# Input projection by stripes of 512 weight columns in a ring of weight pairs, with two token slots instead of three

## The chip, the cores and the metric

One core of a Trainium2 chip runs the whole kernel in one launch. The metric is the time on the device in microseconds; smaller is better. TensorE is called PE, VectorE DVE, ScalarE ACT, GpSimd POOL, and SyncE, which issues most DMAs, SP.

## What is computed

One inference step of a hybrid trunk: a layer norm, one wide input projection of 2064 prompt rows (16 learned meta rows and 2048 tokens) and of 8 x 16 sample rows, two token mixers, gates and an output projection. Cut to what matters:

```python
(g_q, g_k, g_v, g_low, g_r, d_q, d_k, d_v, i_q, i_k, i_w, d_z, m_a, m_b) = jnp.split(
    h @ w_in, SPLIT_OFFSETS, axis=-1)             # h: rows x 1024, w_in: 1024 x 8280
...
log_f = jax.nn.log_sigmoid(g_low @ gla_w2 + gla_gate_b) / GLA_TAU
o_a, s_t = gla_recurrence(q, k, v, log_f, s0)     # linear attention, 4 heads
y_a = (rms_norm(o_a) * jax.nn.silu(g_r)) @ w_gla
...
k_i = layer_norm(i_k, idx_kn_g, idx_kn_b)
o_b = attend(q_d, q_i, w_i, k_d, v_d, k_i)        # index scores choose the 256 best keys, 16 heads
y_b = (o_b * jax.nn.silu(d_z)) @ w_dsa
merged = jax.nn.sigmoid(m_a + gate_b[0]) * y_a + jax.nn.sigmoid(m_b + gate_b[1]) * y_b
h_new = layer_norm(ALPHA * h + merged @ w_out, ln_g, ln_b)
```

Everything is fp32. The matmuls of the projections take each operand as a pair `hi`, `lo` of fp32r tiles (`hi` the rounded value, `lo` the rest), and make three products per contraction tile: hi·hi, hi·lo and lo·hi.

## The kernel before, in words

**Phase 1** (`phase1`, L549) holds the tokens as six pieces of three tiles of 128 (`PIECES`; the first has the 16 meta rows and two tiles, the last ends with the sample tile `s`). `phase_keys` (L356) normalises, transposes and splits each piece into `xh`, `xl` and computes the attention and index keys. Then `project` (L577) runs for three groups of two pieces, [4, 5], [2, 3] and [0, 1]. A group loads its pieces back from DRAM where they are not in a slot any more (L581 to L587: four raw loads of two contraction tiles each; a cast to `xh` on ACT and a subtraction to `xl` on POOL, in `split_sb`, L234). The slots are three pools `xp0` to `xp2`; the list `slots` (L568) says which piece takes which, and `xtiles` (L385) takes the next entry.

Within a group the 1024 x 256 **stripes** of `w_in` follow each other. `weights` (L239) loads a stripe in four raw loads, casts each to `whi` (ACT, L158) and subtracts to `wlo` (POOL, L143); `whi` and `wlo` hold all eight contraction tiles and have two buffers each, `raw` has three. Two kinds of product use them:

- weight-stationary, `stripe_t` (L389) with `tsp` (L304): 128 weight columns are stationary, a piece of 256, 272 or 384 tokens moves. For iq, gq, gk, q, ma and mb; written out by `evac` on ACT or DVE.
- token-stationary, `natural` (L591) with `nat` (L295): a token tile is stationary, the 256 weight columns move. For gv, gr and z.

A product has 24 matmuls (`mm3`, L260, lines 264 to 266). A group has two iq stripes, then 26 steps in the order of `order`; the tiles' index scores (`index_block`, L432, L444 and L445 on PE, reading `iq` from DRAM) come ahead of each set of steps, and the selections on DVE (`select`) at a later priority beside them. `flip` reverses the order of the pieces in the last stripe of the second group.

**Phase 2** (`phase2`, L1233) is attention, linear attention, the merge and the output. Linear attention's gates (`gla_gates`, L652) and the attention of the sample (`attend_sample`, L1122) are side work: its first `NEARLY` = 13 items are issued at a priority 1500 earlier, beside the end of phase 1, as far as their memory is free. The pools of phase 2 lie in SBUF over those that phase 1 leaves, the slots `xp` among them. A scheduler orders the instructions of each engine by these priorities and a model of the timeline, and so the final order isn't to be read off the source alone.

Of the kernel before, what the change touches and what calls it, by code (L numbers as in the profile page):

```python
# [21 lines left out]
P = 128  # L22
# [59 lines left out]
PMAX = 3 * P  # L82
SCW = KT * 300
# [35 lines left out]
class Trunk:  # L119
    def __init__(self, tc, i, o):  # L120
        self.tc, self.nc, self.i, self.o = tc, tc.nc, i, o
        self.turn = 0
        self.spare = self.flip = False
# [106 lines left out]
    def raw(self, n):  # L230
        t = self.ws.tile([P, 2 * PMAX], F32, name="raw", bufs=3)
        return t[:, : 2 * n].rearrange("p (k c) -> p k c", k=2)
# [6 lines left out]
    def weights(self, parts, pool=None, name="", eng=None):  # L239

        nc = self.nc
        width = sum(n for _, n in parts)
        w = self.i["w_in"][0].rearrange("(k p) c -> p k c", p=P)
        if pool is None:
            hi = self.ws.tile([P, KT, width], F32R, name="whi")
            lo = self.ws.tile([P, KT, width], F32R, name="wlo")
        else:
            hi = pool.tile([P, KT, width], F32R, name="whi" + name, tag="sc")
            lo = pool.tile([P, KT, width], F32R, name="wlo" + name, tag="sc")
        for q in range(4):  # L250
            s = slice(2 * q, 2 * q + 2)
            raw = self.raw(width)
            a = 0
            for c, n in parts:
                nc.sync.dma_start(raw[:, :, a : a + n], w[:, s, c : c + n])
                a += n
            self.split_sb(hi[:, s, :], lo[:, s, :], raw, eng)
        return hi, lo
# [36 lines left out]
    def nat(self, x, c, r, w):  # L295

        ps = self.pp.tile([P, 512], F32, name="pp")
        (hi, lo), (xh, xl) = w, x
        n = hi.shape[-1]
        self.mm3(ps[:r, :n], lambda k: xh[:, k, c : c + r], lambda k: xl[:, k, c : c + r],  # L300
                 lambda k: hi[:, k, :], lambda k: lo[:, k, :], KT)
        return ps[:r, :n]

    def tsp(self, x, c, n, w, a):  # L304

        ps = self.pp.tile([P, 512], F32, name="pp")
        (hi, lo), (xh, xl) = w, x
        self.mm3(ps[:, :n], lambda k: hi[:, k, a : a + P], lambda k: lo[:, k, a : a + P],
                 lambda k: xh[:, k, c : c + n], lambda k: xl[:, k, c : c + n], KT)
        return ps[:, :n]  # L310
# [78 lines left out]
    def stripe_t(self, g, c0, width, meta, evac):  # L389
        w = self.weights([(c0, width)])  # L390
        for q in GROUPS[g][:: -1 if self.flip else 1]:
            s = META if q == 0 and not meta else 0
            for a in range(0, width, P):
                evac(c0 + a, self.tsp(self.x[q], s, PCN[q] - s, w, a), PC0[q] + s, PCN[q] - s)
# [154 lines left out]
    def phase1(self):  # L549
        nc, tc, i = self.nc, self.tc, self.i  # L550
        with ExitStack() as c:
# [7 lines left out]
            self.xp = [c.enter_context(tc.tile_pool(name=f"xp{q}", bufs=1)) for q in range(3)]  # L559
# [9 lines left out]
            self.x, self.slots = {}, [0, 1, 2, 0, 1, 2, 0, 1, 2, 1]  # L569
# [7 lines left out]
    def project(self, g):  # L577
# [10 lines left out]
        for q in range(2):  # L588
            self.stripe_t(g, C_IQ + 256 * q, 256, False, self.ev_split("ih", "il", C_IQ))

        def natural(col, dst, base, meta, evac):  # L591
            w = self.weights([(col, 256)])
            for t, q in tiles:
# [5 lines left out]
                evac(e[:r, :256], ps)  # L599
                nc.sync.dma_start(self.d[dst][COL[t] : COL[t] + r, col - base : col - base + 256], e[:r, :256])  # L600
# [4 lines left out]
        def silu_norm(e, ps):  # L605
            self.act(e, ps, AF.Silu)
            self.tt(e, e, self.gng[:], OP.mult, eng=nc.gpsimd)
# [3 lines left out]
            "gq": (2, lambda c: st(g, C_GQ + c, 256, False, self.ev_act("gq", C_GQ, AF.Copy, scale=P ** -0.5))),  # L611
            "gk": (2, lambda c: st(g, C_GK + c, 256, True, self.ev_act("gk", C_GK, AF.Copy))),
            "gv": (4, lambda c: natural(C_GV + c, "gv", C_GV, True, self.copy)),
            "q": (4, lambda c: st(g, C_DQ + c, 256, False, self.ev_heads)),
            "gr": (4, lambda c: natural(C_GR + c, "gr", C_GR, False, silu_norm)),
            "z": (4, lambda c: natural(C_DZ + c, "z", C_DZ, False, silu)),
            "ma": (4, lambda c: st(g, C_MA + c, 256, False, self.ev_act("ma", C_MA, AF.Sigmoid, biascol=0))),
            "mb": (4, lambda c: st(g, C_MB + c, 256, False, self.ev_act("mb", C_MB, AF.Sigmoid, biascol=8))),
        }
        order = ("gr", "z", "ma", "mb", "gk", "gv", "gq", "q") if g == len(GROUPS) - 1 else ("gq", "gk", "gv", "q", "gr", "z", "ma", "mb")  # L620
        def step(n, c):

            self.spare = g == len(GROUPS) - 1 and n in SPARE

            self.flip = g == len(GROUPS) - 2 and (n, c) == (order[-1], 256 * (kinds[n][0] - 1))
            kinds[n][1](c)
            self.spare = self.flip = False

        steps = [lambda n=n, c=256 * q: step(n, c) for n in order for q in range(kinds[n][0])]
# [837 lines left out]
```

## Time and profile before

| | us |
|---|---|
| median of 3 runs | 3671.09 (3671.04 to 3673.03) |
| profiled execution, its own time | 3667.11 |
| its span, first to last instruction | 3665.3 |
| PE busy | 3534.5 (96%) |
| DVE busy | 2570.0 (70%) |
| ACT busy | 1454.6 (40%) |
| POOL busy | 1050.9 (29%) |
| mean granted TensorE clock | 0.985 |

How to read it: busy times are of the profiled execution alone, and a PE that is busy is not one at its peak, since matmuls overlap: two rows of a timeline can overlap, and the price of a matmul in a dense stretch is the distance from start to start. The granted clock is told as a share of full speed. In the program the keys take the first 160 us, the three groups run to about 765, 1345 and 1885 us, and attention follows.

### The profile page before, as it was taken

To read this page: it belongs to the slowest core of one execution; us is meant where nothing else is said; L and a number is where in the kernel's file an instruction comes from. 1 tells how busy PE (TensorE), PEld (TensorE's weight loads), DVE (VectorE), ACT (ScalarE), POOL (GpSimd) and SP (SyncE) were. 2 spreads that over 40 slices of the span, in tenths; PEclk is the share of its full clock that TensorE was granted. 3 is DMA by queue.
4 is the path that set the end of the run, shared out by engine and by line. 5 is a ranking of instruction groups with operands and counts; after the bars stand their busy time and mean duration, and the time that the engine had idled before them with its cause. 6 is when DMAs were issued, how large, how long until landed. Compare 5 with 4: busy or idle time off the path is not lost.

```text
span 3665.3 us, 66399 instructions
## 1 busy us (share of the span) xinstructions
PE 3534.5 (96%) x24484; PEld 3244.8 (89%) x24484; DVE 2570.0 (70%) x5965; ACT 1454.6 (40%) x3084; POOL 1050.9 (29%) x1220
## 2 busy tenths in 40 slices
PE   7999999999999999999999999999999999989999
PEld 7999999999999998998987778777777888879998
DVE  7747997799999998943237777777765665554444
ACT  4444223433334234325334555555665443431110
POOL 3122343242333244334201433333420000012221
PEclk9999999999999999999999999999999999999999
DMA  8642443263442345464554323233343335564431
GB/s 262 198 127 83 136 125 95 83 180 106 123 125 81 109 143 159 124 169 128 134 159 116 96 82 90 81 89 88 85 110 87 103 99 142 150 192 141 122 114 62
DMA packets 530085, 448.82 MB, mean 122 GB/s; under 512 B 87152, under 2 KB 502000, under 8 KB 529760
## 3 DMA queue, kind: packets, MB, share of 16 engines
q1 hardware_dynamic: 529760, 444.58, 42.3%
q8 instruction: 193, 3.16, 0.4%
q14 instruction: 132, 1.08, 0.1%
HBM read 288.01 MB, written 156.44 MB: 121 GB/s over the span
## 4 chain that ended last, share of the span: by engine, by line
PE 75%; DVE 13%; DMA 5%; ACT 2%; issue 2%; POOL 1%; SPq 0%; POOLq 0%; DVEq 0%; ACTq 0%
PE pp L266 12%; PE pp L264 12%; PE pp L265 12%; PE oo L1070 6%; PE px L1046 5%; PE pd L264 3%; PE pd L265 3%; PE pd L266 3%; PE pl L1110 2%; PE pl L1111 2%; DVE lgl L1112 2%; PE fo L264 1%; PE fo L265 1%; PE fo L266 1%; DVE junk L149 1%
## 5 line engine op out<-in xcount | busy, mean ns | idle before, releaser
L143 POOL TENSOR_TENSOR wlo<-raw,whi 128x512 fp32r<-128x512 f32 x360 | 489.1, 1379 | 796.3 <-ACT whi L158 741.0
L149 DVE TENSOR_SCALAR_CACHE_REDUCE junk<-sc,cand 128x272 bf16<-128x272 f32 (+6 forms) x512 | 701.7, 1371 | 17.0
L264 PE MATMUL pp<-xh,whi 128*128 128x384 f32 (+2 forms) x1728 | 566.8, 328 | 1.5 <-ACT whi L158 1.3
L265 PE MATMUL pp<-xl,whi 128*128 128x384 f32 (+2 forms) x1728 | 565.9, 328 | 0.0
L266 PE MATMUL pp<-xh,wlo 128*128 128x384 f32 (+2 forms) x1728 | 565.4, 328 | 0.0
L266 PE MATMUL pp<-whi,xl 128*128 128x256 f32 (+3 forms) x1952 | 559.9, 288 | 5.6 <-DVE xl L143 5.6
L264 PE MATMUL pp<-whi,xh 128*128 128x256 f32 (+3 forms) x1952 | 560.3, 288 | 3.1 <-ACT whi L158 2.2
L265 PE MATMUL pp<-wlo,xh 128*128 128x256 f32 (+3 forms) x1952 | 560.2, 287 | 0.0
L266 PEld LDWEIGHTS pp<-whi,xl 128*128 128x128 f32 (+1 forms) x1952 | 369.9, 190 | 15.4 <-DVE xl L143 7.5
L264 PEld LDWEIGHTS pp<-whi,xh 128*128 128x128 f32 (+1 forms) x1952 | 370.7, 190 | 11.0 <-issue 3.0
L265 PEld LDWEIGHTS pp<-wlo,xh 128*128 128x128 f32 (+1 forms) x1952 | 370.6, 190 | 5.3 <-issue 2.3
L1112 DVE CUSTOM_DVE_ANT_0 lgl<-pl,mkl 128x348 f32<-128x348 f32 (+8 forms) x608 | 297.1, 510 | 84.4 <-PE pl L1111 52.9
L264 PE MATMUL pd<-xh,wh 128*128 128x242 f32 (+3 forms) x1152 | 327.1, 284 | 9.4 <-ACT wh L1324 4.3
L264 PEld LDWEIGHTS pp<-xh,whi 128*128 128x128 f32 x1728 | 327.4, 189 | 3.2 <-ACT whi L158 1.9
L1110 PE MATMUL pl<-kd,q 128*128 128x348 f32 (+14 forms) x800 | 304.2, 383 | 27.0 <-DVE mx L1112 22.3
L265 PEld LDWEIGHTS pp<-xl,whi 128*128 128x128 f32 x1728 | 327.6, 190 | 0.6
L266 PEld LDWEIGHTS pp<-xh,wlo 128*128 128x128 f32 x1728 | 327.0, 189 | 1.3 <-POOL wlo L143 0.6
L265 PE MATMUL pd<-xl,wh 128*128 128x242 f32 (+3 forms) x1152 | 323.9, 281 | 0.6 <-DVE mx L1114 0.3
L266 PE MATMUL pd<-xh,wl 128*128 128x242 f32 (+3 forms) x1152 | 323.6, 281 | 0.0
L155 ACT ACTIVATE lgl<-lgl,mx 128x1040 f32<-128x1040 f32 (+7 forms) x256 | 250.1, 977 | 174.9 <-DVE mx L1114 168.4
L158 ACT CAST whi<-raw 128x512 fp32r<-128x512 f32 (+1 forms) x344 | 199.4, 623 | 300.0 <-DMA raw<-in_w_in 188.8
L1118 POOL COPY pmeta<-lgl 128x48 f32<-128x48 f32 x256 | 58.8, 230 | 766.0 <-ACT lgl L155 761.1
(250 smaller groups left out, 7881.4 us busy)
## 6 DMA issues: line engine op xcount, KB each, us to landing
raw<-in_w_in SPq DMA_DIRECT2D x360, 256.0 KB, 3.2
q<-d_q SPq DMA_DIRECT2D x272, 128.0 KB, 3.0
d_h<-x SPq DMA_DIRECT2D x17, 512.0 KB, 3.3
d_gv<-en SPq DMA_DIRECT2D x68, 128.0 KB, 2.0
d_gr<-en SPq DMA_DIRECT2D x68, 128.0 KB, 1.9
d_z<-en SPq DMA_DIRECT2D x68, 128.0 KB, 1.7
v<-d_gv SPq DMA_DIRECT2D x17, 512.0 KB, 3.9
gr<-d_gr SPq DMA_DIRECT2D x17, 512.0 KB, 4.1
```

The costliest lines, as they stand in the source:

```text
L143: (eng or self.nc.vector).tensor_tensor(out, a, b, op=op)
L149: (eng or self.nc.vector).tensor_scalar(out, a, s1, s2, op0=op0, op1=op1, **kw)
L155: self.nc.scalar.activation(out, a, f, **kw)
L158: (self.nc.vector.tensor_copy if self.spare else self.nc.scalar.copy)(out, src)
L264: mm(ps, ah(k), bh(k), start=k == 0, stop=False)
L265: mm(ps, ah(k), bl(k), start=False, stop=False)
L266: mm(ps, al(k), bh(k), start=False, stop=k == n - 1)
L1046: nc.tensor.transpose(ps[:, 2 * s + u, :], pe[u][a // KLOW][:, a % KLOW : a % KLOW + P], self.ident[:])
L1070: self.nc.tensor.matmul(oo[0][64 * o : 64 * o + 64, k : k + 2, :], self.v[:, s0 + s, d : d + 64], t[:, 2 * s : 2 * s + 2], start=self.fres ...
L1110: nc.tensor.matmul(ps[:, :m], q[:, u, :], kd, start=True, stop=False)
L1111: nc.tensor.matmul(ps[:, :m], q[:, 2 + u, :], kd, start=False, stop=True)
L1112: nc.vector.tensor_tensor_reduce(lg[z1][:, a : a + m], ps[:, :m], mk[z1][:, a : a + m], 1.0, NEG, OP.add, OP.max, mx[:, s : s + 1])
```

## The change

`STRIPE` = 512 columns instead of 256, so each group has one iq stripe and 14 steps. `whi` and `wlo` are no longer whole stripes: `weights` returns pairs of contraction tiles (2 of 8, 512 columns), each in one of `RING` = 6 places, so that a stripe takes four of six. A raw buffer holds 2 x 512 columns instead of 2 x 384, and there are four instead of three. The token slots are two, taken in turn, and `flip` is gone. Products and their values are the same; a natural product is 512 columns wide, in one PSUM bank as before.

```diff
+STRIPE = 512
+RING = 6
+RAWB = 4
...
     def raw(self, n):
-        t = self.ws.tile([P, 2 * PMAX], F32, name="raw", bufs=3)
+        t = self.ws.tile([P, 2 * STRIPE], F32, name="raw", bufs=RAWB)
         return t[:, : 2 * n].rearrange("p (k c) -> p k c", k=2)
...
     def weights(self, parts, pool=None, name="", eng=None):
...
-        if pool is None:
-            hi = self.ws.tile([P, KT, width], F32R, name="whi")
-            lo = self.ws.tile([P, KT, width], F32R, name="wlo")
...
+        pairs = []
         for q in range(4):
...
-            self.split_sb(hi[:, s, :], lo[:, s, :], raw, eng)
-        return hi, lo
+            if pool is not None:
+                hi, lo = (t[:, s, :] for t in whole)
+            else:
+                hi, lo = (self.ws.tile([P, 2, STRIPE], F32R, name="w" + x, bufs=RING)[:, :, :width] for x in ("hi", "lo"))
+            self.split_sb(hi, lo, raw, eng)
+            pairs.append((hi, lo))
+        return (lambda k: pairs[k // 2][0][:, k % 2, :]), (lambda k: pairs[k // 2][1][:, k % 2, :]), width
...
     def stripe_t(self, g, c0, width, meta, evac):
         w = self.weights([(c0, width)])
-        for q in GROUPS[g][:: -1 if self.flip else 1]:
+        for q in GROUPS[g]:
...
-            self.xp = [c.enter_context(tc.tile_pool(name=f"xp{q}", bufs=1)) for q in range(3)]
+            self.xp = [c.enter_context(tc.tile_pool(name=f"xp{q}", bufs=1)) for q in range(2)]
...
-            self.x, self.slots = {}, [0, 1, 2, 0, 1, 2, 0, 1, 2, 1]
+            self.x, self.slots = {}, [0, 1] * 5
...
-        for q in range(2):
-            self.stripe_t(g, C_IQ + 256 * q, 256, False, self.ev_split("ih", "il", C_IQ))
+        self.stripe_t(g, C_IQ, STRIPE, False, self.ev_split("ih", "il", C_IQ))
 
         def natural(col, dst, base, meta, evac):
-            w = self.weights([(col, 256)])
+            w = self.weights([(col, STRIPE)])
...
-            "gr": (4, lambda c: natural(C_GR + c, "gr", C_GR, False, silu_norm)),
+            "gr": (2, lambda c: natural(C_GR + c, "gr", C_GR, False, silu_norm)),
...
-            self.flip = g == len(GROUPS) - 2 and (n, c) == (order[-1], 256 * (kinds[n][0] - 1))
```

The lines of the changed kernel are numbered 5 to 7 higher behind `weights` and 3 higher in the helpers.

**ACT at the end of the first group**, `ea` being the evicted `mb` products, `xh` the cast of piece 3 into slot 1, `whi` the next group's first weights. Before:

```order
L155 ACTIVATE ea_8519<-pp_8494,gateb_2374 128x384
L155 ACTIVATE ea_8547<-pp_8522,gateb_2374 128x384
L158 CAST xh_8912<-raw_8914 128x768
L158 CAST xh_8912<-raw_8918 128x768
L158 CAST xh_8912<-raw_8922 128x768
L155 ACTIVATE ea_8575<-pp_8550,gateb_2374 128x384
L158 CAST xh_8912<-raw_8926 128x768
L158 CAST whi_8930<-raw_8932 128x512
L155 ACTIVATE ea_8603<-pp_8578,gateb_2374 128x384
```

The same place in the changed kernel:

```order
L158 ACTIVATE ea_7372<-pp_7347,gateb_2371 128x384
L158 ACTIVATE ea_7400<-pp_7375,gateb_2371 128x384
L161 CAST xh_7709<-raw_7711 128x768
L161 CAST xh_7709<-raw_7715 128x768
L161 CAST xh_7709<-raw_7719 128x768
L161 CAST xh_7709<-raw_7723 128x768
L161 CAST whi_7729<-raw_7727 128x1024
L161 CAST whi_7735<-raw_7733 128x1024
```

Before, two evictions of the group stand behind the first casts of piece 3, the last of them (`ea_8603`) behind the first weight cast. Now all evictions of the group (`ea_7400` is the last) stand ahead of the casts, and all four casts ahead of the weights.

**PE where the first gates enter** (`pg` is a gate's PSUM tile, `gl` the low-rank gate input). Before, with 1008 projection matmuls into `pp` still to come:

```order
L264 MATMUL pp_18348<-whi_18190,xh_14992 128x256
L265 MATMUL pp_18348<-wlo_18191,xh_14992 128x256
L266 MATMUL pp_18348<-whi_18190,xl_14993 128x256
L666 MATMUL pg_20199<-gl_20195,w2_20130 128x512
L666 MATMUL pg_20203<-gl_20195,w2_20130 128x512
L264 MATMUL pp_18394<-whi_18376,xh_14974 16x256
```

In the changed kernel, with 69 to come:

```order
L272 MATMUL pp_16180<-xl_12590,whi_16003 128x384
L273 MATMUL pp_16180<-xh_12589,wlo_16004 128x384
L671 MATMUL pg_16709<-gl_16705,w2_16640 128x512
L671 MATMUL pg_16713<-gl_16705,w2_16640 128x512
L271 MATMUL pp_16180<-xh_12589,whi_16003 128x384
L272 MATMUL pp_16180<-xl_12590,whi_16003 128x384
```

The gates have moved from the middle of the last group, between `gr`, `z` and `gv` products, to its last `q` products. The sample's attention has moved behind the last projection matmul.

**ACT at the end of the projection in the changed kernel**, `ge` being the gates, `lgl` the logits of the first attention block, `eh` the eviction of the last projection product:

```order
L158 ACTIVATE eh_16267<-pp_16242 128x384
L158 ACT_TABLE_LOAD
L158 ACTIVATE ge_16738<-ge_16738 128x1024
...
L158 ACTIVATE ge_16779<-pg_16784,gb_16642 128x512
L158 ACT_TABLE_LOAD
L158 ACTIVATE ge_16779<-ge_16779 128x1024
...
L158 ACTIVATE ge_16798<-ge_16798 128x1024
L158 ACT_TABLE_LOAD
L158 ACTIVATE lgl_17793,sums_17788<-lgl_17793,mx_17795 128x1040
```

Behind the last eviction now stand the end of the gate tile `ge_16738` and the whole of `ge_16749`, `ge_16768`, `ge_16779` and `ge_16798`, and only then the first exponential of the attention. Before, all gates stood ahead of the projection's end.

## Rows read from the trace of the kernel before

**Rows 1.** The page: busy time of each engine, and the chain that ended last.

```profile
PE 3534.5 (96%) x24484; PEld 3244.8 (89%) x24484; DVE 2570.0 (70%) x5965; ACT 1454.6 (40%) x3084; POOL 1050.9 (29%) x1220
...
PE 75%; DVE 13%; DMA 5%; ACT 2%; issue 2%; POOL 1%; SPq 0%; POOLq 0%; DVEq 0%; ACTq 0%
```

**Rows 2.** Stretches: from:to, length, busy PE, PEld, DVE, ACT, POOL, clock, DMA share, GB/s.

```profile
160.00:755.00 595.00, 589.25 (x3960) 584.80 (x3959) 458.61 (x619) 218.54 (x467) 180.96 (x152) 1.00 0.37 109
...
1678.00:1885.00 207.00, 207.00 (x1434) 185.66 (x1433) 58.78 (x146) 99.60 (x161) 61.63 (x42) 0.94 0.48 133
...
1950.00:2700.00 750.00, 711.34 (x4773) 580.55 (x4772) 562.96 (x1989) 417.79 (x889) 265.43 (x422) 0.98 0.32 89
```

**Rows 3.** Groups of PE by form: count | busy, mean ns | idle before.

```profile
L264 PE MATMUL pp<-whi,xh 128*128 128x256 f32 x1632 | 462.6, 283 | 0.0
```

**Rows 4.** Timeline of PE, matmuls of 256 columns: start, duration, instruction [idle before].

```profile
505.29 0.28 PE L265 MATMUL pp<-wlo,xh 128*128 128x256 f32 x1
...
506.49 0.28 PE L266 MATMUL pp<-whi,xl 128*128 128x256 f32 x1
```

**Rows 5.** Timeline of PE, matmuls of 512 columns in the output projection.

```profile
3419.62 0.39 PE L266 MATMUL fo<-woh,mgl 128*128 128x512 f32 x1
...
3421.20 0.39 PE L264 MATMUL fo<-woh,mgh 128*128 128x512 f32 x1
```

**Rows 6.** Timeline of ACT at the end of the first group.

```profile
771.95 0.58 ACT L155 ACTIVATE ea<-pp,gateb 128x384 f32<-128x384 f32 x1 [3.58 <-PE pp L266]
772.43 2.30 ACT L158 CAST xh<-raw 128x768 fp32r<-128x768 f32 x3
...
778.38 0.84 ACT L158 CAST xh<-raw 128x768 fp32r<-128x768 f32 x1 [1.69 <-DMA raw<-d_xt]
780.12 0.62 ACT L158 CAST whi<-raw 128x512 fp32r<-128x512 f32 x1 [0.90 <-DMA raw<-in_w_in]
```

**Rows 7.** Timeline of POOL at the same place.

```profile
779.30 1.82 POOL L143 TENSOR_TENSOR xl<-raw,xh 128x768 fp32r<-128x768 f32 x1 [0.51 <-ACT xh L158]
781.09 2.54 POOL L143 TENSOR_TENSOR wlo<-raw,whi 128x512 fp32r<-128x512 f32 x2
```

**Rows 8.** Timeline of PE, the next group's first matmul.

```profile
780.79 0.44 PE L264 MATMUL pp<-xh,whi 128*128 128x384 f32 x1 [0.60 <-ACT whi L158]
```

**Rows 9.** The page, DMA issues: count, KB each, us to landing.

```profile
raw<-in_w_in SPq DMA_DIRECT2D x360, 256.0 KB, 3.2
```

**Rows 10.** Timeline of PE, index scores behind the second group's end.

```profile
1388.33 0.57 PE L444 MATMUL pi<-kih,iq 128*128 128x272 f32 x1 [5.69 <-DMA iq<-d_il]
```

**Rows 11.** Groups of PE by form between 1678 and 1885 us, gates and sample.

```profile
L1195 PE MATMUL pg<-spt,vb 128*64 128x32 f32 x160 | 18.3, 241 | 0.0
L666 PE MATMUL pg<-gl,w 16*128 16x512 f32 x32 | 17.7, 636 | 0.0
L1193 PE MATMUL pg<-pn,vn 16*64 16x32 f32 x80 | 12.5, 237 | 0.0
L1157 PE MATMUL pg<-ident,kn 128*128 128x128 f32 x48 | 9.1, 303 | 0.0
```

**Rows 12.** Timeline of PE behind the sample's products, projection matmuls of 256.

```profile
1868.89 0.41 PE L265 MATMUL pp<-xl,whi 128*128 128x256 f32 x1
1869.10 0.41 PE L266 MATMUL pp<-xh,wlo 128*128 128x256 f32 x1
```

**Rows 13.** Timeline of ACT, a half chunk of gates.

```profile
1680.75 0.69 ACT L155 ACTIVATE ge<-pg,gb 128x512 f32<-128x512 f32 x1 [45.90 <-PE pg L666]
...
1682.32 1.28 ACT L155 ACT_TABLE_LOAD   x1
1683.61 1.06 ACT L155 ACTIVATE ge<-ge 128x1024 f32<-128x1024 f32 x1
```

**Rows 14.** Timelines: the last projection matmul on PE, the first attention exponential on ACT.

```profile
1884.97 0.34 PE L266 MATMUL pp<-xh,wlo 128*128 128x384 f32 x1
1897.07 1.17 ACT L155 ACTIVATE lgl<-lgl,mx 128x1040 f32<-128x1040 f32 x1 [0.49 <-DVE smx L1173]
```

More of the change, by code (lines that the diff above doesn't have):

```diff
@@ L122, in __init__ @@
         self.turn = 0
-        self.spare = self.flip = False
+        self.spare = False
     @contextmanager
@@ L243, in weights @@
         w = self.i["w_in"][0].rearrange("(k p) c -> p k c", p=P)
-        if pool is None:
-            hi = self.ws.tile([P, KT, width], F32R, name="whi")
-            lo = self.ws.tile([P, KT, width], F32R, name="wlo")
-        else:
-            hi = pool.tile([P, KT, width], F32R, name="whi" + name, tag="sc")
-            lo = pool.tile([P, KT, width], F32R, name="wlo" + name, tag="sc")
+        if pool is not None:
+            whole = [pool.tile([P, KT, width], F32R, name="w" + x + name, tag="sc") for x in ("hi", "lo")]
+        pairs = []
         for q in range(4):
@@ L256, in weights @@
                 a += n
-            self.split_sb(hi[:, s, :], lo[:, s, :], raw, eng)
-        return hi, lo
+            if pool is not None:
+                hi, lo = (t[:, s, :] for t in whole)
[4 more added lines that the diff above has]
+        return (lambda k: pairs[k // 2][0][:, k % 2, :]), (lambda k: pairs[k // 2][1][:, k % 2, :]), width
     def mm3(self, ps, ah, al, bh, bl, n):
@@ L297, in nat @@
         ps = self.pp.tile([P, 512], F32, name="pp")
-        (hi, lo), (xh, xl) = w, x
-        n = hi.shape[-1]
+        (hi, lo, n), (xh, xl) = w, x
         self.mm3(ps[:r, :n], lambda k: xh[:, k, c : c + r], lambda k: xl[:, k, c : c + r],
-                 lambda k: hi[:, k, :], lambda k: lo[:, k, :], KT)
+                 hi, lo, KT)
         return ps[:r, :n]
@@ L306, in tsp @@
         ps = self.pp.tile([P, 512], F32, name="pp")
-        (hi, lo), (xh, xl) = w, x
-        self.mm3(ps[:, :n], lambda k: hi[:, k, a : a + P], lambda k: lo[:, k, a : a + P],
+        (hi, lo, _), (xh, xl) = w, x
+        self.mm3(ps[:, :n], lambda k: hi(k)[:, a : a + P], lambda k: lo(k)[:, a : a + P],
                  lambda k: xh[:, k, c : c + n], lambda k: xl[:, k, c : c + n], KT)
@@ L598, in natural @@
                 e = self.ev.tile([P, 512], F32, name="en", tag="ev")
[L599 to L600 removed]
+                evac(e[:r], ps)
+                nc.sync.dma_start(self.d[dst][COL[t] : COL[t] + r, col - base : col - base + STRIPE], e[:r])
         def silu(e, ps):
@@ L606, in silu_norm @@
             self.act(e, ps, AF.Silu)
-            self.tt(e, e, self.gng[:], OP.mult, eng=nc.gpsimd)
+            h = e.rearrange("p (h d) -> p h d", d=256)
+            self.tt(h, h, self.gng[:, None, :].to_broadcast(list(h.shape)), OP.mult, eng=nc.gpsimd)
         st = self.stripe_t
         kinds = {
[L611 to L614, printed above, removed]
-            "gr": (4, lambda c: natural(C_GR + c, "gr", C_GR, False, silu_norm)),
-            "z": (4, lambda c: natural(C_DZ + c, "z", C_DZ, False, silu)),
-            "ma": (4, lambda c: st(g, C_MA + c, 256, False, self.ev_act("ma", C_MA, AF.Sigmoid, biascol=0))),
-            "mb": (4, lambda c: st(g, C_MB + c, 256, False, self.ev_act("mb", C_MB, AF.Sigmoid, biascol=8))),
+            "gq": (1, lambda c: st(g, C_GQ + c, STRIPE, False, self.ev_act("gq", C_GQ, AF.Copy, scale=P ** -0.5))),
+            "gk": (1, lambda c: st(g, C_GK + c, STRIPE, True, self.ev_act("gk", C_GK, AF.Copy))),
+            "gv": (2, lambda c: natural(C_GV + c, "gv", C_GV, True, self.copy)),
+            "q": (2, lambda c: st(g, C_DQ + c, STRIPE, False, self.ev_heads)),
+            "gr": (2, lambda c: natural(C_GR + c, "gr", C_GR, False, silu_norm)),
+            "z": (2, lambda c: natural(C_DZ + c, "z", C_DZ, False, silu)),
+            "ma": (2, lambda c: st(g, C_MA + c, STRIPE, False, self.ev_act("ma", C_MA, AF.Sigmoid, biascol=0))),
+            "mb": (2, lambda c: st(g, C_MB + c, STRIPE, False, self.ev_act("mb", C_MB, AF.Sigmoid, biascol=8))),
         }
@@ L623, in step @@
             self.spare = g == len(GROUPS) - 1 and n in SPARE
-            self.flip = g == len(GROUPS) - 2 and (n, c) == (order[-1], 256 * (kinds[n][0] - 1))
             kinds[n][1](c)
-            self.spare = self.flip = False
-        steps = [lambda n=n, c=256 * q: step(n, c) for n in order for q in range(kinds[n][0])]
+            self.spare = False
+        steps = [lambda n=n, c=STRIPE * q: step(n, c) for n in order for q in range(kinds[n][0])]
         blocks = [t for t, _ in tiles if t not in ("m", "s", 0)]
```

## The prediction

> **What bounds the kernel now.** I read the page first: TensorE is busy 96% of the span, no other engine above 70%, and the chain of waits runs through PE for 75%, DVE for 13% [rows 1]. Then the busy time by stretch: the input projection is PE without holes (589.25 of 595 us in a stretch of the first group), its last 207 us are PE alone, busy for all 207, and attention behind it still has PE busy 711 of 750 us while DVE stands at 563 [rows 2]. So the change is worth what it takes off PE, less the holes it opens. The groups by line and the timelines then give the price of one matmul at each width, and the timelines of ACT, POOL and PE round a group's end the price of a late token slot. I call T the end of the last projection matmul (1885.0 us before). About 0.2%, 7.3 us, is what a measurement tells from no change.
>
> **1. Wider natural products: −32.5.** The token-stationary products (gr, z, gv) move 256 weight columns past each token tile. The trace has 1632 of them per line [rows 3], and 32 more for the 16 meta rows (eight contraction tiles in each of four gv stripes), so 1664 x 3 = 4992 matmuls become 2496 of 512. A matmul of 256 starts 0.120 us after the one ahead (ten steps in 1.20 us) [rows 4], one of 512 in the output projection 0.227 (seven steps in 1.58 us) [rows 5]. A pair merged saves 2 x 0.120 − 0.227 = 0.013 us, x 2496 = 32.5, all of it on the path since PE has no holes there. Bounds: 25 to 40, by ±0.003 in the difference. The weight-stationary products keep their widths and count.
>
> The Trainium skill, "TensorE: Matmul & The Clock Gate", section "Back-to-back issue gap", speaks against this: an isolated gap grows as N/2.4 ns plus only 2.5 ns. By it a merged pair saves 2.5 ns, 6 us in all. The same section gives about 131 ns as the sustained spacing at 512, which would save far more. The rows here agree with neither figure: 0.227 at 512 and 0.120 at 256 leave 13 ns a pair.
>
> **2. Two slots: group ends, +19.5.** Before, a flipped piece order frees slot 1 two accumulations ahead of the group's end. The chain at the first such end: the last reader's eviction at 771.95, three casts of 0.77 on ACT right behind it and the fourth at 778.38, the first weight cast at 780.12 [rows 6], the `xl` subtractions on POOL 1.82 each [rows 7], and PE starts the next group at 780.79 after 0.60 us of idleness [rows 8]. From the freed slot to PE's start it is 9 us, of which PE covers nearly all; with what it waits just behind I count 1.2 us lost per end. In the change the slot is freed by the group's last matmul, and the order of ACT puts all four casts of piece 3 ahead of the first weight cast. The same 9 us are then bare; the cast grows to 1.06 (0.62 at 512 elements, 0.84 at 768), and the first `wlo` stands behind 4 x 1.82 on POOL plus a subtraction of twice 1.27, so about 11.5 us after the end. PE has products with `whi` between the two. Per end 9 to 12, I take 11, less 1.2, for two ends +19.5 (bounds 15.5 to 21.5). What makes it late is SP as well: a weight load takes the raw buffer of the first `xl` subtraction and lands 3.2 us after issue [rows 9]. In the keys phase two slots cost nothing: a slot is free some 20 us before its reuse there.
>
> **3. Ring of six: +5.** A stripe holds four places, so the next stripe's pairs 0 and 1 are ready ahead, but its pairs 2 and 3 wait for the running stripe's pairs 0 and 1, read to the end by its last accumulation. From the release: an eviction and a cast on ACT, 1.6 us, two subtractions of 2.55 on POOL in series [rows 7], with hand-offs some 4.9 us to pair 2 and 7.5 to pair 3. By PE's order the first use lies 5.7 to 6.9 and 7.2 to 8.3 us behind the release. That is 0 to 1.5 us of slack at some 39 stripe ends (45 stripes, less the first of each group and those behind index blocks). POOL also holds `sc` memsets behind DVE's selections and the `gng` product. Bounds 0 to 39 x 0.7 = 27; I take 5, being nearest to the slack. Weight bytes stay the same: 180 loads of 512 KB instead of 360 of 256 [rows 9].
>
> **4. Index scores: −3.** At 1388 us PE waits 5.69 us for `iq` from `d_il` [rows 10], because the second stripe of 256 index columns has just been written. With one stripe of 512 all heads of the first piece come first. Bounds −5.7 to 0.
>
> **5. Gates and sample attention move out of the projection: +10.** This part the diff does not tell; the order does. Their memory lies where slot 0 was free through the last group. Before, the gates enter PE with 1008 projection matmuls to go; in the change with 69, and sample attention after T. In the 207 us behind 1678 the two cost PE 18 + 40 = 58 us (the four largest groups alone 57.6, counting matmuls that overlap; small groups fill the rest) [rows 11], and the granted clock is 0.94 [rows 2]: around the thin fp32 products a 256-wide matmul steps by 0.21 instead of 0.12 [rows 12]. At 1.00 these 207 us would give back 207 x 0.06 = 12, some 11 of it on projection matmuls. So T comes 69 us earlier. The 58 come back in attention, at the same price where PE stays the bound. And the ramp into attention gets a hole. Each half of a gate chunk holds ACT for 2 x 0.69 + 1.28 + 1.06 + 1.28 + 1.06 = 6.1 us [rows 13]; before, all ten were done by 1745. In the change four still stand on ACT between T and the first attention exponential, which so moves from T+12 [rows 14] to T+12+24 = T+36. PE has only part of this filled: by its order it finds about 37 us of work up to where it had done 55, so +18. Dips of the clock that now fall on attention cost 0 to 11, I take 3. Sum −69 + 58 + 18 + 3 = +10. Bounds: −20, if the moved work falls into half of attention's 39 us of PE idleness and DVE's slack [rows 2] and the ramp hole closes; +30, with the hole at 24, all the dips, and 6 of new waits.
>
> **6. Chunks of linear attention run one block later: +2** (0 to 5), as the merge of the last blocks loses cover. The wider POOL and ACT instructions are fewer by half and lie beside PE: nothing, as POOL is busy 29% [rows 1].
>
> **Sum:** −32.5 + 19.5 + 5 − 3 + 10 + 2 = +1. The profiled execution took 3667.1 and would take 3668; the median of the runs stands 4 us above it (3671.09), so **3672**.
>
> **The rivals.**
> - A, the sum, within its own bounds of about ±14: 3658 to 3686, chance 0.42; 0.22 of that within 0.2% of before, 0.10 on each side.
> - B, faster: the moved work is absorbed. For it speaks the idle PE and DVE of attention [rows 2]; against it, that ACT is in order with the gates ahead of the exponentials. Term 5 at −10 instead of +10 gives 3652. Chance 0.25.
> - C, slower: the ramp is bare. If PE fills none of the four half chunks on ACT, 24 us are lost, and with all the dips term 5 is −69 + 58 + 24 + 11 = +24, with term 2 at its upper bound 21.5: +17, so 3688. It decides if the first exponential comes later than T+30 with PE idle for more than 20 us of it. Chance 0.22.
> - D, slower: the ring runs dry. If each of the 39 ends loses 0.7 us, term 3 is 27 and the time 3694. It decides once a subtraction on POOL is later by more than 1 us at most ends. Chance 0.08.
> - E, slower: nothing saved by the wider matmul, which steps by twice 0.120 here as no load of weights can hide; term 1 is 0 and the time 3705. Against it stand the 0.227 of [rows 5], which have the same weight load per matmul. Chance 0.03. By the gap rule of the Trainium skill named under 1 it would be 3698.
>
> **How the numbers follow.** Likeliest is A: 3672. Faster is B and 0.10 of A, 0.35; within 0.2% 0.22; slower C, D, E and 0.10 of A, 0.43. Cases of both signs hold most of the chance, so A's own range is 3658 to 3686; that for 8 in 10 reaches to the middle of B and beyond C and D: 3642 to 3702.
>
> **What would show it.** Right: matmuls of 512 into `pp` at 0.227; PE idle near 10 us at two group ends, ended by ACT `whi` or POOL `wlo`; under 0.3 us idle on average at stripe ends; a granted clock near 1.00 to the projection's end, near 1805 (1885 − 32.5 − 69 + 19.5 + 5 − 3); a first attention exponential near T+36. Wrong: a hole at every stripe end (D), or attention no longer than before although it now holds the sample (B).

## The result, and the profile after

The changed kernel takes 3729.44 us (median of four runs, 3725.34 to 3730.65), 1.0158 times the time before (95% interval 1.0146 to 1.0171): 58 us slower. The forecast was 3672, with 3642 to 3702 for eight in ten. T, the end of the last projection matmul, is 1860.3 instead of the 1805 that was worked out, and from T to the last matmul it is 1860 us instead of 1772 before.

The page of the changed kernel, busy times and chain (before: [rows 1]):

```profile
PE 3531.8 (95%) x21988; PEld 3136.2 (84%) x21988; DVE 2638.7 (71%) x5941; ACT 1424.8 (38%) x2824; POOL 991.6 (27%) x1006
...
PE 43%; DVE 23%; DMA 4%; issue 3%; ACT 3%; SPq 1%; POOL 0%; DVEq 0%; POOLq 0%; ACTq 0%
```

DVE is busy 69 us longer with 24 instructions fewer, and its share of the chain has gone from 13% to 23%, PE's from 75% to 43%. So some of DVE's instructions take longer. The stretches by stage, first the second group of the kernel before (a row that the prediction had not looked at), then the changed kernel's second group, the first part of its third, and the way into attention:

```profile
780.80:1354.00 573.20, 562.19 (x3720) 556.42 (x3720) 546.44 (x838) 197.58 (x404) 199.75 (x160) 0.99 0.41 119
```

```profile
784.50:1368.20 583.70, 556.42 (x2848) 514.96 (x2848) 552.90 (x813) 187.06 (x306) 174.26 (x87) 0.98 0.37 116
1368.20:1660.00 291.80, 271.54 (x1524) 247.83 (x1525) 251.02 (x484) 86.42 (x141) 108.22 (x53) 0.96 0.46 138
...
1860.00:1950.00 90.00, 68.17 (x338) 46.58 (x337) 39.32 (x120) 70.40 (x101) 17.27 (x15) 0.75 0.44 128
```

In the second group DVE was busy for 546 of 573 us before: PE at 562 was the busiest, but DVE was only 16 us behind it. Now the group takes 584 us, ten more, with PE six less busy. The granted clock, 0.99 there before, is 0.98, and 0.96 in the third group.

The widened matmuls behave as forecast. The timeline of PE has nine steps in 2.04 us, 0.227 each (before, half as wide: [rows 4]):

```profile
505.15 0.39 PE L272 MATMUL pp<-wlo,xh 128*128 128x512 f32 x1
...
507.19 0.39 PE L272 MATMUL pp<-wlo,xh 128*128 128x512 f32 x1
```

Where PE waited in the projection, the view of waits for PE: us in total, times, longest. The kernel before:

```profile
PE pi L444 <- DMA iq<-d_il: 11.4, 4, 5.7
PE pi L444 <- ACT rl L155: 10.0, 12, 2.0
...
PE pp L264 <- ACT whi L158: 3.4, 4, 1.3
```

The changed kernel:

```profile
PE pi L450 <- ACT rl L158: 27.4, 13, 4.9
PE pp L271 <- ACT whi L161: 18.2, 3, 8.0
PE pp L271 <- DVE el L146: 12.3, 2, 9.7
```

The waits for `whi` are the two group ends (7.90 and 8.01 us, and 2 elsewhere). The waits for `el`, the eviction of the index columns on DVE, and for `rl`, whose buffers DVE's scores free, are new or grown, and both come from DVE. Timelines of PE, DVE and POOL behind the second group's end show one of them:

```profile
1368.21 0.58 PE L271 MATMUL pp<-xh,whi 128*128 128x256 f32 x1 [8.01 <-ACT whi L161]
...
1393.32 0.69 PE L271 MATMUL pp<-xh,whi 128*128 128x384 f32 x1 [9.67 <-DVE el L146]
```

```profile
1370.10 1.02 DVE L152 TENSOR_SCALAR dlt<-cnt 128x3 int32<-128x3 f32 x1
1371.16 2.29 DVE L155 SCALAR_TENSOR_TENSOR cand<-dlt,cand 128x3 int32<-128x3 int32 x1
...
1378.31 2.23 DVE L152 TENSOR_SCALAR dlt<-cnt 128x3 int32<-128x3 f32 x1
1380.57 2.32 DVE L155 SCALAR_TENSOR_TENSOR cand<-dlt,cand 128x3 int32<-128x3 int32 x1
...
1387.74 0.17 DVE L152 TENSOR_SCALAR dlt<-cnt 128x3 int32<-128x3 f32 x1
1387.94 0.16 DVE L155 SCALAR_TENSOR_TENSOR cand<-dlt,cand 128x3 int32<-128x3 int32 x1
...
1392.84 0.75 DVE L146 TENSOR_TENSOR el<-pp,eh 128x256 fp32r<-128x256 f32 x2
```

```profile
1368.72 14.15 POOL L146 TENSOR_TENSOR wlo<-raw,whi 128x1024 fp32r<-128x1024 f32 x6
```

The selection's `dlt` and `cand` work on three numbers per partition. Alone they take 0.17 and 0.16 us; while POOL runs six subtractions of 2.36 us back to back (1368.72 to 1382.87), the four shown take 1.02 to 2.32, together 7.9 us instead of 0.7. `el` stands behind them in DVE's order, and PE waits 9.67 us for it. Of the 120 `cand` of this form, the 90 that start outside any POOL instruction of two tensors take at most 0.17 us each, and the 30 that start inside one 2.07 on average; before it was 94 and 26, and the 26 took 1.23. Over the whole kernel, by groups of DVE (count | busy, mean ns), before and after:

```profile
L152 DVE SCALAR_TENSOR_TENSOR cand<-dlt,cand 128x3 int32<-128x3 int32 x120 | 47.2, 393 | 3.9
```

```profile
L155 DVE SCALAR_TENSOR_TENSOR cand<-dlt,cand 128x3 int32<-128x3 int32 x120 | 76.6, 638 | 3.8
```

**Theory P**: the change doubled the length of POOL's subtractions; each holds such DVE instructions for its own length, the selection runs late, and evictions and scores behind it on DVE stop PE. **Rival S**: the loss is that of the two slots and of the side work they displace. **Rival O**, later: another order by the scheduler, since each edit below also moves instructions. A fourth reading is that the longer subtractions only deliver `wlo` later; but PE's waits for POOL's `wlo` are 1.5 us in the changed kernel and 0.7 in run 1, 1.6 in run 7 and none in run 8.

### The profile page after: what moved, and what is told of

It is laid out like the page before. It is cut to its first block, busy times and chain, and to the rows that moved or that the text cites. A ratio compares the mean times of both kernels' runs of the same rounds, so it can differ in the third digit from the quotient of the medians.

```text
span 3728.8 us, 60231 instructions
## 1 busy us (share of the span) xinstructions
PE 3531.8 (95%) x21988; PEld 3136.2 (84%) x21988; DVE 2638.7 (71%) x5941; ACT 1424.8 (38%) x2824; POOL 991.6 (27%) x1006
## 4 chain that ended last, share of the span: by engine, by line
PE 43%; DVE 23%; DMA 4%; issue 3%; ACT 3%; SPq 1%; POOL 0%; DVEq 0%; POOLq 0%; ACTq 0%
DVE junk L152 10%; PE oo L1075 6%; PE px L1051 4%; PE pd L271 3%; PE pd L273 3%; PE pd L272 3%; PE pp L273 2%; PE pp L271 2%; PE pp L272 2%; PE pl L1115 2%; PE pl L1116 2%; DVE cand L155 2%; PE fo L271 2%; PE fo L272 2%; PE fo L273 2%
## 5 line engine op out<-in xcount | busy, mean ns | idle before, releaser
L146 POOL TENSOR_TENSOR wlo<-raw,whi 128x1024 fp32r<-128x1024 f32 x180 | 439.5, 2470 | 737.7 <-PE pp L273 367.5
L273 PE MATMUL pp<-whi,xl 128*128 128x512 f32 (+3 forms) x1120 | 414.2, 371 | 4.7 <-DVE xl L146 4.6
L271 PE MATMUL pp<-whi,xh 128*128 128x512 f32 (+3 forms) x1120 | 412.7, 371 | 3.2 <-ACT whi L161 2.2
L272 PE MATMUL pp<-wlo,xh 128*128 128x512 f32 (+3 forms) x1120 | 413.7, 371 | 0.0
L1115 PE MATMUL pl<-kd,q 128*128 128x348 f32 (+14 forms) x800 | 309.4, 390 | 25.8 <-DVE mx L1117 13.3
L155 DVE SCALAR_TENSOR_TENSOR sc<-rl,iw,sc 128x388 f32<-128x388 f32 (+16 forms) x308 | 229.6, 789 | 78.9 <-ACT rl L158 77.6
L1051 PE MATMUL px<-ident,lgl 128*128 128x128 f32 x1600 | 251.4, 280 | 18.5 <-ACT lgl L158 6.2
L158 ACT ACTIVATE rl<-pi 128x388 f32<-128x388 f32 (+14 forms) x352 | 168.5, 510 | 258.1 <-DVE sc L155 94.0
L1116 PE MATMUL pl<-kd,q 128*128 128x348 f32 (+14 forms) x800 | 266.5, 337 | 0.0
```

What stands on the lines that cost most here:

```text
L146: (eng or self.nc.vector).tensor_tensor(out, a, b, op=op)
L155: self.nc.vector.scalar_tensor_tensor(out, a, s, b, op0=op0, op1=op1)
L158: self.nc.scalar.activation(out, a, f, **kw)
L271: mm(ps, ah(k), bh(k), start=k == 0, stop=False)
L272: mm(ps, ah(k), bl(k), start=False, stop=False)
L273: mm(ps, al(k), bh(k), start=False, stop=k == n - 1)
```

## The experiments

Beside each run stands its ratio to the kernel before with the 95% interval. T and the time from T to the last matmul are read off PE's timeline; the kernel before has 1885.0 and 1772.

### 1. POOL's subtractions in halves

```diff
-        self.tt(lo, src, hi.bitcast(F32), OP.subtract, eng=eng or self.nc.gpsimd)
+        if len(hi.shape) == 2 or eng is not None:
+            self.tt(lo, src, hi.bitcast(F32), OP.subtract, eng=eng or self.nc.gpsimd)
+            return
+        n, c = 1, hi.shape[-1] // 1
+        for k in range(2):
+            for a in range(0, n * c, c):
+                self.tt(lo[:, k, a : a + c], src[:, k, a : a + c], hi[:, k, a : a + c].bitcast(F32), OP.subtract, eng=self.nc.gpsimd)
```

> The changed kernel with each POOL subtraction to wlo and xl in the projection cut in two (one contraction tile each, 512 or 384 wide), all else as it is. Theory P (POOL's longer subtractions hold DVE's short instructions until they end, so selections and scores run late and PE waits for them): the mean of cand<-dlt,cand on DVE falls from 0.63 us to about 0.39 and DVE busy by 40 to 60 us; PE idle before the projection's end falls from 86 us to 55 to 65; time 3695 to 3710. Rival S (the loss is that of the two slots and the moved side work): DVE's instructions may get shorter, but the time stays within 8 us of 3729.

3691.84 us (1.0061, 1.0041 to 1.0080), 38 less than the changed kernel. T is 1819.3, 41 earlier; from T on it is 1863 us as against 1860. A group of DVE, and the waits of PE:

```profile
L155 DVE SCALAR_TENSOR_TENSOR cand<-dlt,cand 128x3 int32<-128x3 int32 x120 | 51.3, 428 | 3.9
```

```profile
PE pp L277 <- ACT whi L161: 17.9, 3, 8.2
PE pi L456 <- ACT rl L158: 15.7, 14, 3.4
...
PE pp L277 <- DVE el L146: 5.8, 1, 5.8
```

The waits for `rl` and `el` fall from 39.7 to 21.5 us; those at the group ends stay. Of the 41 us, 27 are idleness of PE ahead of T (98.3 us before the edit, 71.4 with it) and 14 busy time of PE, at a mean granted clock of 0.99 instead of 0.98 from 160 us to T. DVE is busy 50 us less, as P had it; the mean of `cand` stays a little above P's 0.39, and the time falls 3 us below its range.

### 7 and 8. The mirror: wide subtractions in the kernel before

Run 7 subtracts four contraction tiles at a time from two raw buffers of four tiles; run 8 has the same buffers and subtracts two at a time, as before. The core of run 7; run 8 has `range(0, 4, 2)`, `u + 2` and `4 * q + u + 2` in the last three lines:

```diff
-        t = self.ws.tile([P, 2 * PMAX], F32, name="raw", bufs=3)
+        t = self.ws.tile([P, 4, 256], F32, name="raw", bufs=2).rearrange("p k c -> p (k c)")
...
+                for u in range(0, 4, 4):
+                    s = slice(4 * q + u, 4 * q + u + 4)
+                    self.tt(lo[:, s, :], raw[:, u : u + 4, :], hi[:, s, :].bitcast(F32), OP.subtract, eng=nc.gpsimd)
```

> The kernel before (three slots, stripes of 256, early side work) with POOL subtractions to wlo of 1024 elements, over four contraction tiles at a time, from two raw buffers of four tiles instead of three of two or three. Theory P: the mean of cand<-dlt,cand rises from 0.37 to 0.55 to 0.65 us and DVE busy by 40 to 60 us against the next run, and the time is 10 to 35 us over that of the next run. Rival O: no difference from the next run beyond 5 us.

> The control to the run ahead: the same two raw buffers of four tiles, but the subtractions of 512 elements as in the kernel before. cand<-dlt,cand stays at about 0.37 us on all theories; the time is that of the kernel before plus what the fewer raw buffers cost, 0 to 20 us.

Run 7 3729.64 us (1.0167, 1.0150 to 1.0183), run 8 3677.46 (1.0026, 1.0016 to 1.0036): 52 us for the width alone, in a kernel with three slots, narrow stripes and early side work, more than expected. T differs by 45 (1939.5 and 1894.3). The groups of run 7, then of run 8:

```profile
L152 DVE SCALAR_TENSOR_TENSOR cand<-dlt,cand 128x3 int32<-128x3 int32 x120 | 69.9, 583 | 3.9
```

```profile
L152 DVE SCALAR_TENSOR_TENSOR cand<-dlt,cand 128x3 int32<-128x3 int32 x120 | 47.1, 393 | 3.8
```

One of run 7's new waits shows another way from DVE to PE. Timelines of SP and PE:

```profile
1631.02 0.34 SPq L550 DMA_DIRECT2D d_mask<-eq  x1
...
1631.92 0.93 SPq L255 DMA_DIRECT2D raw<-in_w_in  x2
```

```profile
1636.00 0.69 PE L275 MATMUL pp<-xh,whi 128*128 128x384 f32 x1 [11.42 <-ACT ea L155]
```

SP writes a selection's mask `eq` ahead of the next weight loads and waits 25.4 us for it; ACT's cast waits for the weights, an eviction stands behind the cast, and PE waits 11.42 us for that eviction.

As to rival O: ahead of T the orders of the changed kernel and run 1 differ in 372 of PE's 9640 instructions, those of runs 7 and 8 in 349 of 12530, and T moves by 41 and 45; those of the kernel before and run 4 (below) differ in 575 of 12536, and T moves by 0.5. So in that case a change of order of like extent did not move T. With runs 1, 7 and 8 theory P is shown from both sides: halving the subtractions takes 38 us of the loss out of one kernel, doubling them puts 52 into the other.

### 4 and 5. Narrower still

> The kernel before with each POOL subtraction of the projection cut in two (256 or 384 wide). Theory P: the mean of cand<-dlt,cand falls from 0.39 to about 0.28 us and DVE busy by 15 to 30 us; as PE bounds this kernel the time falls by only 0 to 8 us, to 3663 to 3671. Rival S: the DVE numbers do not move with the width on POOL.

3678.31 us (1.0021, 1.0009 to 1.0033): DVE is busy 39 us less by its page (2531.4), more than expected, T is unchanged (1885.5), and nothing is gained; the 7 to 10 us more lie behind T and were not expected.

> As the first run, but each POOL subtraction of the projection cut in four (256 or 192 wide). Theory P goes on: the mean of cand<-dlt,cand falls below the 0.427 us of the halves to about 0.33, and the projection's end comes 5 to 15 us earlier than their 1819; time 3675 to 3690 against 3692 for the halves. Rival O (the halves were faster because the scheduler wrote another order, not because of the width): cand changes, the time does so by chance in either direction, by more than 10 us perhaps.

3746.17 us (1.0212, 1.0196 to 1.0228): a miss, 54 us slower than halves, although the mean of `cand` fell to 0.322 us as expected. At both group ends one `dlt` was held for some 16 us. Timelines of DVE, POOL and PE:

```profile
786.26 15.80 DVE L152 TENSOR_SCALAR dlt<-cnt 128x3 int32<-128x3 f32 x1
```

```profile
794.37 7.67 POOL L146 TENSOR_TENSOR wlo<-raw,whi 128x256 fp32r<-128x256 f32 x11
```

```profile
813.62 0.69 PE L277 MATMUL pp<-xh,whi 128*128 128x384 f32 x1 [11.03 <-DVE el L146]
```

The instruction ends at 802.06, when POOL's run of short subtractions ends (802.04). Two such holds give PE two holes of 11 us; T is 21 later than with halves. The other 30 us lie behind T (1893 instead of 1863), where the code is the same but 2409 of PE's 12348 instructions stand in another order; their cause was not found, and rival O may hold there. So a shorter width is not always faster: in such a run of short subtractions the hold lasted as long as the run, and not as long as one of them.

### 2. Two slots in the kernel before

```diff
-            self.xp = [c.enter_context(tc.tile_pool(name=f"xp{q}", bufs=1)) for q in range(3)]
+            self.xp = [c.enter_context(tc.tile_pool(name=f"xp{q}", bufs=1)) for q in range(2)]
...
-            self.x, self.slots = {}, [0, 1, 2, 0, 1, 2, 0, 1, 2, 1]
+            self.x, self.slots = {}, [0, 1] * 5
...
-        for q in GROUPS[g][:: -1 if self.flip else 1]:
+        for q in GROUPS[g]:
```

> The kernel before with two token slots taken in turn and without flip; stripes of 256 and POOL's instructions as before. Theory P: the slots alone cost the two group ends (+16 to +20) and the moved side work (+10), so 3695 to 3705, with cand<-dlt,cand at 0.39 us. Rival S: they cost all of the loss and the natural saving besides: 3740 to 3765, since the wider stripes would have saved 32.

3717.86 us (1.0128, 1.0113 to 1.0144): 50 more, between the two theories. T is 1838.3, 47 earlier, and from T on it is 1871.5, 100 longer. Group ends idle 9.04 and 8.55 us. Against this run, the changed kernel with halves (run 1), whose subtractions to `wlo` have the same 512 elements, is 26 us faster, 19 of it ahead of T: that is what the wide stripes bring, ring, raw buffers and shorter `xl` subtractions included.

### 3 and 9. The side work alone, with three slots

> The kernel before with no side work issued early (NEARLY = 0): three slots, stripes of 256, and gates and sample attention behind the projection. The prediction's term 5 alone: T comes 65 to 70 us earlier, near 1816, a hole of 15 to 25 us on PE behind it, and in sum 3677 to 3690. Rival S: what is moved costs more in attention than in the projection: over 3700.

> The kernel before with only the five gate chunks issued early (NEARLY = 5); the sample's attention comes behind the projection. Moving all of it cost 49 us (third run), so which part is it? By PE time the sample is 42 of the 62 us that came back after the projection. Theory: each part costs in the proportion of its PE time, so T near 1835 and a time of 3695 to 3705. Rival: the sample, whose work is chains over several engines, can be paced into the attention and is nearly free there, and the gates' table loads on ACT are what costs: 3668 to 3680.

With nothing early 3717.81 us (1.0130, 1.0115 to 1.0145), with the gates alone early 3671.15 (1.0006, 0.9997 to 1.0016). Run 3 came out as its rival S had it, and the theory of proportion fell. Moving the sample brings T forward by 55 (to 1830.0) and takes 56 back: free. Moving the gates as well brings T forward by 18 more, and takes back 70. No ramp hole makes this up, as the first exponential of run 3 is at T+15; what does was not separated.

### 6. The index weights ahead of the second piece

```diff
         for q in GROUPS[g]:
+            if q == GROUPS[g][1]:
+                first = self.weights([(C_IQ, STRIPE)])
...
-        self.stripe_t(g, C_IQ, STRIPE, False, self.ev_split("ih", "il", C_IQ))
+        self.stripe_t(g, C_IQ, STRIPE, False, self.ev_split("ih", "il", C_IQ), first)
```

> The first run's kernel (changed kernel, POOL subtractions in halves), with the weights of a group's index stripe loaded ahead of the group's second piece instead of behind it. If the 8 us holes at the two group ends come from the four casts and subtractions that stand ahead of the weights, as term 2 had it, they shrink to 0 to 2 us, T comes 12 to 16 us earlier and the time is 3675 to 3682. If the slot itself decides, the hole only moves behind the first piece's products and the time stays within 5 us of 3692.

3677.59 us (1.0026, 1.0016 to 1.0035), 14 less than run 1, T 1807.4. No wait over 1.5 us is left at either group end. So the holes there were the order of casts and subtractions ahead of the weights, as term 2 had it.

### 10 to 17. Where gates, sample and loads stand

Runs 10 and 11 are run 6 with NEARLY = 5 and 0.

> The sixth run's kernel (changed kernel, POOL subtractions in halves, weights ahead of the second piece) with NEARLY = 5: only the gates stand ahead of attention, the sample is paced through it. Theory: T stays near 1807, the ramp hole of 16 us on PE stays with the gates; the sample spread over attention costs what it costs now: 3672 to 3684. Rival: the sample standing early was what held attention, and the time falls to 3655 to 3668.

> The same with NEARLY = 0: gates are paced through attention too. Theory: the ramp hole of 16 us goes (first exponential near T+15 as in the third run instead of T+38) but linear attention starts later, and what is gained at the ramp is lost at attention's end, as in the third run, where T to the end was 26 us longer than with the gates early: 3680 to 3710. Rival: the hole was the loss: 3660 to 3670.

3676.57 (1.0028, 1.0017 to 1.0038) and 3692.89 (1.0065, 1.0042 to 1.0088). The sample's place is free here too; gates paced through attention cost 16. Runs 12 to 16 bring the gates back into the projection, by pools in another order: run 12 the changed kernel, 13 and 14 run 6 with NEARLY = 5 and 13, 15 and 16 keep the upper keys' pools at the bottom. That of run 16:

```diff
             upper = [left(f"kdu{q}") for q in range(2)]
+            self.sb = left("sb")
+            gc = self.gla_pools(early)
             self.stu = left("stu")
-            gc = self.gla_pools(early)
+            self.gi = left("gi")
+            self.gm = left("gm", 2)
...
-            self.sb = left("sb")
```

> The changed kernel with only the places of phase 2's left pools reordered (those of the gates first, below the two slots, over index memory that is free earlier), and NEARLY = 5: by its order the gates enter PE with 1049 projection matmuls to go, the sample behind the projection. If the gates behind the projection cost 20 to 27 us in the changed kernel, and the sample nothing (ninth run), this takes 3702 to 3712, with the first attention exponential near T+12 and the projection's end 5 to 15 us later than 1860. Rival: the two slots cost through something else, and the time stays at 3725 to 3735.

> All three repairs together: POOL subtractions in halves, the index stripe's weights ahead of the second piece, gates early and sample late. If their gains add (38 + 14 + 20 to 27 from 3729) it takes 3650 to 3660, faster than the kernel before (3667). If the gates cost as much in the projection as behind it: 3670 to 3680.

> The same with NEARLY = 13, where by the order most of the sample's products (192 of 242 rows) lie in the projection too. By the ninth run the sample costs the same in either place: within 8 us of the run ahead. Rival: around the sample's thin products the clock falls in the projection, and it is 8 to 15 us slower than the run ahead.

> As the thirteenth run (all three repairs, gates early, sample late), but the upper keys' places and the probabilities' pool stay at the bottom, below the gates' pools: by its order the gates enter with 927 projection matmuls to go, and the upper keys' loads stand 140 rows earlier on SP than there. If the ramp (first attention exponential at T+30 instead of T+12 although the gates were early) came from the attention's loads standing behind the projection, it shrinks to T+12 to T+20 and the time to 3662 to 3674. If the ramp is the sample's products ahead of attention, it stays near T+30 and the time near 3684.

> The same with the probabilities' pool above the gates' instead of below, gates with 1041 matmuls to go. The mask loads of the first block are 20 rows later on SP and 10 behind the sixth run's. Same theories: 3662 to 3676 if the keys' loads made the ramp, near 3684 if not.

3734.25 (1.0183, 1.0163 to 1.0203), 3684.23 (1.0038, 1.0023 to 1.0053), 3689.87 (1.0062, 1.0048 to 1.0076), 3693.25 (1.0078, 1.0063 to 1.0093) and 3675.71 (1.0019, 1.0007 to 1.0032): run 12 came out as its rival had it, run 14 lies within 8 us of run 13 as expected, runs 13 and 15 missed, and run 16 reached its time without the shorter ramp that was to bring it. In run 13 T is 22 later than in run 10 and the rest 15 shorter, so the gates' place was worth nothing. The first exponential stays at T+28 to T+38 in all five, though the gates were done before T. In run 16 SP issues the first block's loads only some 18 us after T (1821), by its timeline:

```profile
1838.75 0.47 SPq L1019 DMA_DIRECT2D mkl<-d_mask  x1
1839.26 2.71 SPq L174 DMA_DIRECT2D q<-d_q  x4
```

> The second run's kernel (two slots, stripes of 256, 3718) with the gates' pools ahead of the probabilities' pool and NEARLY = 5: by its order 1008 projection matmuls stand behind the first gates, as in the kernel before, and the first mask loads on SP stand where the ninth run has them. If the ramp (first exponential T+41 in the second run) is the gates behind the projection, it falls to T+12 to T+18 and the time to 3688 to 3698, leaving the two group ends (about 20 us) as what the slots cost. If it is the loads of attention, held by something else, the ramp stays above T+28 and the time above 3705.

3701.36 us (1.0087, 1.0059 to 1.0114), between both: 16 less than run 2, with the first exponential still at T+38. So with two slots a ramp of 28 to 41 us stands behind the projection whether the gates are early or not, and in runs 3 and 9, with three, one of 12 to 15. What goes with it in every trace is the first block's mask load on SP, which run 16's line above has behind T (1821) and the kernel before ahead of it (1885):

```profile
1876.04 0.38 SPq L1007 DMA_DIRECT2D mkl<-d_mask  x1
```

In all six kernels with three slots it is issued 8 to 11 us ahead of T, with the first exponential at T+12 to T+20; in all thirteen with two slots 14 to 22 us behind T, with the exponential at T+28 to T+41. No run moves this load alone, so that it makes the ramp is not shown. No version was found that beats the kernel before; runs 6, 10 and 16 come within 0.3% of it.

## Why the prediction was wrong

- **What failed first, in term 6: "The wider POOL and ACT instructions are fewer by half and lie beside PE: nothing, as POOL is busy 29% [rows 1]."** PE hardly waits for POOL (1.5 us for `wlo`), but DVE does, and in the second group DVE was busy only 16 us less than PE. Halving POOL's subtractions gives back 38 us of time and 41 of T (run 1); doubling them in the kernel before costs 52 (run 7 against 8). No rival named this; C and D, which were to hold the slower side, have other mechanisms.
- **The Trainium skill**, "SBUF — State Buffer", section "Who interferes with whom", says that a DVE instruction with two SBUF inputs contends with a GpSimd instruction that reads SBUF, and its section "SBUF: two separate sides" that whichever starts first gets the shared pair for the whole instruction. By that rule a subtraction of twice the length holds such an instruction up to twice as long, which is the mechanism of theory P. The trace agrees: `cand`, with two inputs, is held up to 2.35 us beside subtractions of 2.36, up to 1.28 beside those of 1.25 to 1.27 (run 1), and `junk`, whose one large input is `sc`, has the same mean in both kernels, as the largest form shows (before, then after, where nine of the 32 start while POOL works). The rule on two inputs does not cover `dlt`, which reads one tensor and was held up to 2.32 us as well, nor the holds over many subtractions in runs 1 and 5.

```profile
L149 DVE TENSOR_SCALAR_CACHE_REDUCE junk<-sc,cand 128x2064 bf16<-128x2064 f32 x32 | 75.6, 2362 | 1.0
```

```profile
L152 DVE TENSOR_SCALAR_CACHE_REDUCE junk<-sc,cand 128x2064 bf16<-128x2064 f32 x32 | 75.6, 2361 | 1.0
```

- **Term 1, −32.5, was right in its step**, 0.227 us. What the wide stripes bring in time, run 1 against run 2, is −26 where terms 1, 3 and 4 have −30.5. Rival E is out. So are the 2.5 ns a pair of the gap rule of the Trainium skill, "TensorE: Matmul & The Clock Gate", section "Back-to-back issue gap": 0.227 us against twice 0.120 leaves 13 ns.
- **Term 2, +19.5, was right in mechanism and near in size**: 7.90 and 8.01 us idle instead of 9 to 12 a group end, and run 6 gets 14 back by the order of loads alone.
- **Term 3, +5, was too much, and rival D did not come**: by groups, before any product of 512 and before the 384-wide products with `wlo`, PE idles 0.0 and 0.1 us; what idles is at group ends and behind `el`:

```profile
L271 PE MATMUL pp<-xh,whi 128*128 128x384 f32 x1440 | 485.6, 337 | 20.2 <-DVE el L146 12.3 <-ACT whi L161 7.9
...
L273 PE MATMUL pp<-xh,wlo 128*128 128x384 f32 x1440 | 482.7, 337 | 0.1
...
L271 PE MATMUL pp<-whi,xh 128*128 128x512 f32 x816 | 318.7, 393 | 0.0
```

- **Term 4, −3**: the waits for `iq` (11.4 us) are gone, but those for `rl` grew by 17, of which run 1 takes 12 back: DVE again.
- **Term 5, +10, was mis-sized, and this is the second step that failed.** T by the two slots alone is 47 earlier; with the group ends' 20 set aside that is near the forecast 69. Its other half, "58 + 18 + 3" = 79, came out as 100 in run 2 and 89 in the changed kernel. The first exponential was forecast at T+36 and is at T+38.5, with PE waiting for gate inputs and for `q` (timelines of PE, then of ACT):

```profile
1873.04 7.53 PE L671 MATMUL pg<-gl,w 16*128 16x512 f32 x8 [10.49 <-DMA gl<-d_gl]
1886.23 0.63 PE L1115 MATMUL pl<-kd,q 128*128 128x348 f32 x1 [5.67 <-DMA q<-d_q]
```

```profile
1898.79 1.16 ACT L158 ACTIVATE lgl<-lgl,mx 128x1040 f32<-128x1040 f32 x1
```

  The hole of 18 us was about right in the changed kernel: from T to this exponential PE idles 16 of 38.5 us, and behind T in all 19 us more than before (in run 2 26). Rival C asked for more than 20, so it is not C either. The 58 and the dips of the clock, put at 3, were too low: PE is busy 69 us more behind T, in run 2 74. Stretches of the 90 us behind T, the kernel before and run 2 (the changed kernel's, at 0.75, stands above):

```profile
1885.00:1975.00 90.00, 86.84 (x578) 68.88 (x577) 60.13 (x192) 45.24 (x88) 12.80 (x24) 0.92 0.51 145
```

```profile
1838.30:1928.30 90.00, 66.03 (x231) 39.38 (x231) 37.26 (x110) 75.71 (x102) 21.75 (x16) 0.66 0.45 138
```

  In sum two slots cost 50 us (run 2), not the 32 of terms 2, 5 and 6. The sample was priced rightly (run 9: free); how the rest divides between gates, loads and clock stays open.
- **The sum as measured**: two slots +50 (run 2), wide stripes −26 (from run 2 to run 1), POOL's width +38 (from run 1 to the changed kernel). These three follow each other from the kernel before to the changed one, so that they add up to its loss is no further evidence; the changed kernel lies 58 us above the kernel before by the runs of the result, 61 by those beside runs 1 and 2.

## What to carry to other kernels

An engine that is idle 70% of the time can still be the one that matters, through what its instructions hold: before widening an instruction on POOL, look which short DVE instructions run beside it, and whether their chain is close to the bound of the stage. Read the busy time of every engine in each stage, not over the span: 546 of 573 us was there to be seen. Price moved work by the wait in front of its next consumer as well as by its own time, and look in the order at what the freed or taken memory lets start early.

## What the runs showed of the hardware

- A DVE instruction of 128 x 3 numbers took 0.16 us alone and up to 2.33 beside POOL subtractions of 2.36 us (changed kernel).
- Shorter POOL instructions do not always shorten the hold: in a run of twelve of 512 elements one `dlt` took 8.87 us (run 1), in runs of 256-wide ones 15.80 and 16.68 (run 5), each time until POOL's run ended; beside six of 1024 none was held over 2.35.
- After a hole of PE the next matmuls ran at the lower clock: behind the 9.67 us hole at 1393.32 the granted clock is 0.50 (the level of 1.2 GHz) and 384-wide matmuls step by 0.32 us up to 1398.92, then by 0.175; the granted clock of the 90 us behind T is 0.75.
